# Layer 0 projections on fp32 operands in place of pairs of a high and a low part

## The chip, the cores and the metric

The kernel runs on 1 core of a Trainium2 chip. The metric is the device time of one execution in microseconds (us), lower is better. The kernel before was timed in 3 runs.

## What is computed

A trunk of two layers on 1024 tokens of width 1024, all of it fp32. Layer 0 mixes the tokens by sparse attention: each query keeps the 256 keys that a small indexer scores highest, and attends over a low-rank latent of those. Layer 1 mixes them by a gated MLP over chunks of 128 tokens. A SwiGLU block follows each. The change lies at the start of layer 0:

```python
h = modulate(rmsnorm(x, norm_mix_g[layer]), sh1, sc1)
proj = h @ w_in
q     = proj[..., :1024]                 # 8 heads x 128
c_kv  = rmsnorm(proj[..., 1024:1280], g_kv)
q_idx = proj[..., 1280:1792]             # 8 index heads x 64
k_idx = layernorm(proj[..., 1792:1856], g_kidx, b_kidx)
w_idx = proj[..., 1856:1864] * (8 ** -0.5 * 64 ** -0.5)
score = sum over heads of relu(q_idx . k_idx) * w_idx, causal
_, idx = lax.top_k(score, 256)
```

`modulate` scales and shifts h by two vectors that come from a product of the conditioning vector with `mod_w`.

## The kernel before

`trunk` (L111) runs on one core. A scheduler fixes the order of the instructions on each engine; tables at the head of the file give the order in which the source offers them. Tensors lie transposed, features on the 128 partitions: h is 8 tiles k (KT) of 128 features by 1024 tokens, worked on in two chunks `ch` of 512 tokens (CW). Buffers: `pg` has 37 pages of 128x1024 fp32, `wsp` has 8 for weights, `wrp` has 2 (tag `wr`) for raw weights and for the tiles `md` of the conditioning product.

Four projections multiply h, and all use one scheme. A weight tile is loaded raw by `split_w` (L145; SP issues the load, L149). ACT rounds it to a high part in fp32r (L154), and POOL or DVE subtracts to get the low part (L155). `norm_k` (L297) makes h for one k and chunk: DVE multiplies by the reciprocal root (L299), ACT scales and shifts (L301), ACT rounds to the high part (L303), and DVE for even k, POOL for odd k, subtracts for the low part (L304). A product is then three matmuls in `mm3` (L162): high by high (L165), high by low (L166), low by high (L167). "A step" here is one weight tile against one k and one chunk. Low by low is left out.

- **kw**, index keys and index weights, 72 columns: `kw_mm` (L392), 8 x 2 = 16 steps, weight tile `wi`.
- **qi**, index queries, 4 column tiles: `qi_mm` (L396) and the second half of `q_fin` (L427). 8 x 4 = 32 steps of 512 columns for chunk 1, and 32 of 256 columns for chunk 0, whose first 256 tokens keep all their keys. The weight comes in 4 tiles `wqi`.
- **c**, the latent: `ckv_chunk` (L477), 2 x 2 x 8 = 32 steps, weights `wc` (`wc_load`, L440).
- **q**, attention queries: `q_proj` (L460), 8 heads x 2 x 8 = 128 steps, weights `wq` (`q_load`, L450).

The order. BEG (L51) lists the front: loads of x (`x`), statistics (`s`), conditioning dot products (`m`, `mod_dot` L216: a load, then DVE in L232 or POOL in L221), h of chunk 0 and 1 (`a`, `b`), weights (`i`, `q`). There kw and qi run as tiles of h come. Then `idx_scores` (L617) makes index scores of blocks of 128 queries on PE (`lg_ps`, L633 and L634), DVE, ACT and POOL. SEQ (L41) mixes them with two groups of top-256 searches, `search` (L680). A search halves an interval again and again: DVE and ACT count scores above a threshold (L692, L690), DVE adds up and sets the next one (L694, L695); a high half of the bits, ending in `hikey`, comes ahead of a low half. FO (L42) lists the side work, q and c. `pump` (L520) deals it out between the index scores by RATE (L44), and what is left runs after them, mixed with `k_ps` and `v_ps` (keys and values of a head from the latent). The attention follows (`s_ps`, the scores), which needs the searches' results as a mask (`bias`, L750), then the output projection and the rest of the trunk, all of it with `mm3` or its like.

Of the kernel before, what the change touches and what calls it, by code (L numbers as in the profile page):

```python
# [8 lines left out]
F32 = mybir.dt.float32  # L9
# [10 lines left out]
P = 128  # L20
D = 1024
T = 1024
KT = 8
CW = 512
# [30 lines left out]
QWR = 1  # L55
SQPL = ((1, 2),)
PIN = 1
# [53 lines left out]
def trunk(ctx, tc, xT, c, modT, vec, kgb, w_idx, w_q, w_a, wuk, wuv, wo, wg, wu, wd,  # L111
          bwu, bwv, bwo, bws, bbs, outT):
    nc = tc.nc
    PE, DVE, ACT, POOL, SP = nc.tensor, nc.vector, nc.scalar, nc.gpsimd, nc.sync

    cst = ctx.enter_context(tc.tile_pool(name="cst", bufs=1))
    pg = ctx.enter_context(tc.tile_pool(name="pg", bufs=37))
    wrp = ctx.enter_context(tc.tile_pool(name="wrp", bufs=2))
    wsp = ctx.enter_context(tc.tile_pool(name="wsp", bufs=8))
# [6 lines left out]
    def page(name, dt=F32):  # L126
        return pg.tile([P, 1024], dt, name=name, tag="pg")

    def t2(name, dt=F32):
        return tmp.tile([P, CW], dt, name=name, tag="t2")  # L130

    def pa(name):
        return psa.tile([P, CW], F32, name=name, tag="pa")
# [4 lines left out]
    def hl(name, full=False):  # L138
        t = pg.tile([P, 2, CW], F32R, name=name, tag="pg")
        return (t[:, 0, :], t[:, 1, :], t) if full else (t[:, 0, :], t[:, 1, :])  # L140

    def f(ap):
        return ap.bitcast(F32)

    def split_w(src, n, name, pool=None, eng=None, rpool=None, pin=False):  # L145
        pl_, tag = pool or (wsp, "ws")
        rp, rtag = rpool or (wrp, "wr")
        r = rp.tile([P, 1024], F32, name=name + "r", tag=rtag)
        d = SP.dma_start(r[:, :n], src)  # L149
        if pin:  # L150
            tc.keep_in_program_order(d)
        h = pl_.tile([P, 1024], F32R, name=name + "h", tag=tag)
        l = pl_.tile([P, 1024], F32R, name=name + "l", tag=tag)
        ACT.copy(h[:, :n], r[:, :n])  # L154
        (eng or DVE).tensor_sub(l[:, :n], r[:, :n], f(h[:, :n]))  # L155
        return h, l

    def kslices(hl, n, w=P):
        h, l = hl
        return [(h[:, k * w:(k + 1) * w], l[:, k * w:(k + 1) * w]) for k in range(n)]  # L160

    def mm3(ps, st, mv, first, last, run=False):  # L162
        sh, sl = st
        mh, ml = mv
        PE.matmul(ps, sh, mh, start=first, stop=False, skip_group_check=run)  # L165
        PE.matmul(ps, sh, ml, start=False, stop=False, skip_group_check=run)  # L166
        PE.matmul(ps, sl, mh, start=False, stop=last, skip_group_check=run)  # L167
# [44 lines left out]
    modv = [cst.tile([P, 48], F32, name=f"modv{l}") for l in range(2)]  # L212
    asc = [[cst.tile([P, KT], F32, name=f"asc{l}{s}") for s in range(2)] for l in range(2)]
# [41 lines left out]
    def rstd_bcast(xs, n_feat, acc=None, sqs=None, mid=None, pp=None, sqp=None, bst=BST, order=range(KT)):  # L255
        pp = pp or pb
        st = pp("st")
        if sqp is not None:
            acc, sqs = sqp
            xs = [xs[k] for k in order]  # L260
            sqs = [sqs[k % len(sqs)] for k in range(KT)]
        elif acc is None:
            acc = t2("acc")
        for k, x in enumerate(xs):
            if k == 0:
                ACT.activation(acc, x, AF.Square)
            else:
                sq = sqs[k] if sqs else t2("sq")
                ACT.activation(sq, x, AF.Square)
                DVE.tensor_add(acc, acc, sq)  # L270
        v = sm.tile([P, 8], F32, name="var")
        for b in range(4):
            pe_st = PE.matmul(st[:, b:b + 1], acc[:, b * P:(b + 1) * P], ones[:, 0:1], start=True, stop=True)
        if mid is not None:
            next(mid)
        DVE.tensor_scalar(v[:, :4], st[:, :4], 1.0 / n_feat, EPS, op0=ALU.mult, op1=ALU.add)
        y = rsqrt_small(v[:, :4], 4)
        rb = pp("rb")
        if bst:
            for b in range(4):  # L280
                pe_rb = PE.matmul(rb[:, b * P:(b + 1) * P], y[:, b:b + 1].to_broadcast([P, P]), ident, start=True, stop=True)
            pe_chain[:] = [pe_st, pe_rb]
            return rb
        dg = tmp.tile([P, CW], F32, name="dg", tag="wt", bufs=2) if DGW else t2("dg")
        DVE.tensor_mul(dg.rearrange("p (b t) -> p b t", b=4), ident[:, None, :].to_broadcast([P, 4, P]),
                       y[:, :4, None].to_broadcast([P, 4, P]))
        pe_rb = PE.matmul(rb, ones, dg, start=True, stop=True)
        pe_chain[:] = [pe_st, pe_rb]
        return rb
# [4 lines left out]
        h = [sqpg[c][:, i * CW:(i + 1) * CW] for c in (ch, 2) for i in range(2) if c in sqpg]  # L294
        return h[0], [h[1]] + ([h[2 + ch]] if len(h) > 2 else [])

    def norm_k(x, rb, a, sh, k):  # L297
        xr = t2("xr")
        DVE.tensor_mul(xr, x, rb)  # L299
        h = t2("hf")  # L300
        ACT.activation(h, xr, AF.Identity, scale=a[:, k:k + 1], bias=sh[:, k:k + 1])  # L301
        hi, lo = hl("h")
        ACT.copy(hi, h)  # L303
        (POOL if k % 2 else DVE).tensor_sub(lo, h, f(hi))  # L304
        return hi, lo

    def norm_chunk(xp, ch, a, sh):
        cs = slice(ch * CW, ch * CW + CW)
        rb = rstd_bcast([x[:, cs] for x in xp], D)
        return [norm_k(xp[k][:, cs], rb, a, sh, k) for k in range(KT)]  # L310

    x0 = [page("x0") for _ in range(KT)]
    rbs = page("rbs")
    acc0 = page("acc0")
    sq0 = [page("sq0") for _ in range(2)]
# [3 lines left out]
    def x_load(ch):  # L319
        for k in range(KT):  # L320
            SP.dma_start(x0[k][:, ch * CW:(ch + 1) * CW], xT[k, :, ch * CW:(ch + 1) * CW])
# [39 lines left out]
    wis, wqi = [], [None] * KT  # L361
    h0 = [[None] * KT for _ in range(2)]
    with tc.issue_after(silu.ins):
        sq_table()
    for t in BEG:
        if t[0] == "x":
            x_load(int(t[1]))
        elif t[0] == "s":
            x_stat(int(t[1]))
        elif t[0] == "c":  # L370
            c_load()
        elif t[0] == "m":
            mod_first(int(t[1]))
        elif t[0] in "ab":
            k, ch = int(t[1]), int(t[0] == "b")
            cs = slice(ch * CW, ch * CW + CW)
            h0[ch][k] = norm_k(x0[k][:, cs], rbs[:, cs], asc[0][0], modv[0][:, 0:8], k)
        elif t[0] == "i":
            wis += kslices(split_w(w_idx, 8 * 72, "wi", pool=(pg, "pg"), rpool=(pg, "pg")), KT, 72)
        else:  # L380
            hl_ = split_w(w_q[int(t[1])], 1024, "wqi", eng=POOL, pool=(pg, "pg"), rpool=None if QWR else (pg, "pg"))
            wqi[2 * int(t[1]):2 * int(t[1]) + 2] = [kslices((hl_[0][:, q * CW:(q + 1) * CW], hl_[1][:, q * CW:(q + 1) * CW]), 4) for q in range(2)]
    kwp = [psa.tile([P, CW], F32, name="kw_ps", tag="pa") for _ in range(2)]
    qip = {(i, 0): pa("qi_ps") for i in range(QPA)}
    for i in range(4):
        qip[i, 1] = pb("qi_ps")
    Q0 = 256

    def q_in(hlk, ch):
        return [t[:, Q0:] for t in hlk] if ch == 0 else hlk  # L390

    def kw_mm(k):  # L392
        for ch in range(2):
            mm3(kwp[ch][:72], wis[k], h0[ch][k], k == 0, k == KT - 1)

    def qi_mm(i, ch, k):  # L396
        n = CW if ch else CW - Q0
        mm3(qip[i, ch][:, :n], wqi[k][i], q_in(h0[ch][k], ch), k == 0, k == KT - 1)

    for k in range(KT):  # L400
        if k < KWF:
# [4 lines left out]
    for k in range(KWF, KT):  # L406
        kw_mm(k)
# [19 lines left out]
    def q_fin():  # L427
        for (i, ch), p in qip.items():
            for k in range(K1, KT):
                qi_mm(i, ch, k)  # L430
            q_out(i, ch, p)
        for i in range(QPA, 4):
            p = pa("qi_ps")
            for k in range(KT):
                mm3(p[:, :CW - Q0], wqi[k][i], q_in(h0[0][k], 0), k == 0, k == KT - 1)
            q_out(i, 0, p)

    wc = []

    def wc_load():  # L440
        wc[:] = [kslices(split_w(w_a[8 + i], 1024, "wc", eng=POOL, pin=PIN), KT) for i in range(2)]

    q_d = drm.tile([NH, P, T], F32, name="q_d")
    o_d = drm.tile([NH, P, T], F32, name="o_d")
# [3 lines left out]
    WQ = {}  # L448

    def q_load(h):  # L450
        if h < NH:
            WQ[h] = kslices(split_w(w_a[h], 1024, "wq", eng=POOL, pin=PIN and h == 0), KT)

    gate = [None]

    def pe_step(p, w, mv, k):
        with (tc.issue_after(gate[0].ins) if gate[0] is not None else ExitStack()):
            mm3(p, w[k], mv[k], k == 0, k == KT - 1)

    def q_proj(h):  # L460
        w = WQ[h]
# [79 lines left out]
    if QF:  # L541
        q_fin()
    knat = page("knat")
    kn = knat[:, :NB * 72].rearrange("p (b d) -> p b d", b=NB)
    for ch in range(2):
        p = pa("kn_ps")
# [5 lines left out]
    mv = cst.tile([P, NB, 2], F32, name="mv")  # L552
# [21 lines left out]
    for ch in range(2):  # L574
        p = pa("kT_ps")
# [22 lines left out]
    for qbs in ((3, 2, 1, 0), (5, 4), (7, 6)):  # L598
        t = pg.tile([P, 2048], BF16, name="bias", tag="pg")
        o = 0  # L600
        for qb in qbs:
            bias[qb] = t[:, o:o + (qb + 1) * P]
            n = wide.get(qb, (qb + 1) * P)
# [4 lines left out]
    for qb in range(2):  # L608
        n = (qb + 1) * P
# [947 lines left out]
    for ch in F1:  # L1557
        if ch is None:
            continue
        cs = slice(ch * CW, ch * CW + CW)  # L1560
        rb = rstd_bcast([x[:, cs] for x in x1], D, sqp=sq_get(ch), order=SQO[ch], pp=pa, bst=FB[ch])
# [4 lines left out]
        for k in range(KT):  # L1566
            o = page("o")[:, :CW]
            x, fg = x1[k][:, cs], V[:, V_FIN + k:V_FIN + k + 1]
# [69 lines left out]
```

## Time and profile before

| | |
|---|---|
| 3 runs: median (lowest to highest) | 2643.21 us (2641.03 to 2648.29) |
| the profiled execution: its time, its span | 2644.98 us, 2643.0 us |
| PE, PE weight loads, DVE, ACT, POOL busy | 90%, 73%, 83%, 47%, 53% of the span |
| granted PE clock, mean | 0.948 of full speed |
| DMA | 328.65 MB, mean 124 GB/s |

The shares are means over stages with different limits. The part up to about 575 us is layer 0's attention, where the change is; the rest is the output projection, layer 1 and the two SwiGLU blocks. An fp32r matmul of 512 columns shows a duration of some 0.39 us but the next one starts 0.23 us later: they are pipelined, and the spacing is the cost. One core runs, so there is no other core to compare with.

### The profile page before, as it was taken

The numbers are of one execution on the slowest core, as the hardware profiler recorded it, in microseconds if no ns is written. First come the engines' busy times: TensorE is split into PE (matmuls) and PEld (weight loads), VectorE is DVE, ScalarE is ACT, GpSimd is POOL, SyncE is SP. The second block draws the span as 40 slices with busy tenths as digits, with TensorE's granted clock in tenths as the row PEclk, the third lists the DMA queues.
The fourth block names the chain that finished last, engine by engine and source line by source line (L and its number), as shares of the span: only waits on it lengthen the run. The fifth ranks groups of instructions, "written<-read, shape, count | busy, mean of one in ns | idle before, by whom it ended". The sixth has DMA issues, their size and how long they took to land.

```text
span 2643.0 us, 31759 instructions
## 1 busy us (share of the span) xinstructions
PE 2375.1 (90%) x10542; PEld 1934.4 (73%) x10542; DVE 2191.0 (83%) x3457; ACT 1245.9 (47%) x2278; POOL 1399.1 (53%) x993
## 2 busy tenths in 40 slices
PE   6979688998889999899988989988998999998996
PEld 5757577776677888777766877866776888886785
DVE  7799988799898887799879688899878656569986
ACT  5577785655533333343355454533454333333334
POOL 4342243365755554656646556575466444456663
PEclk7989788999899999999999999988989999998998
DMA  6001265645264453631122343363132222253121
GB/s 244 26 32 70 98 206 159 222 143 164 73 223 159 164 179 136 239 136 56 56 96 71 110 145 124 126 255 127 48 112 92 96 76 92 76 209 134 40 96 64
DMA packets 133924, 328.65 MB, mean 124 GB/s; under 512 B 14080, under 2 KB 30720, under 8 KB 133760
## 3 DMA queue, kind: packets, MB, share of 16 engines
q1 hardware_dynamic: 130432, 318.22, 34.5%
q0 software_dynamic: 3328, 8.39, 1.1%
q8 instruction: 84, 1.38, 0.2%
q14 instruction: 80, 0.66, 0.1%
HBM read 253.16 MB, written 73.40 MB: 124 GB/s over the span
## 4 chain that ended last, share of the span: by engine, by line
PE 44%; DVE 27%; issue 6%; DMA 6%; ACT 3%; POOL 2%; SPq 0%; DVEq 0%; POOLq 0%; ACTq 0%
PE p L1194 8%; PE p L1195 8%; PE p L1196 8%; PE d_ps L165 3%; PE d_ps L167 3%; PE d_ps L166 3%; DVE x L944 3%; DVE wst L1050 2%; DVE gm L1050 2%; DVE ms L957 1%; DVE md L232 1%; DVE wst L1174 1%; DVE sqp L270 1%; DMA zg<-z_d 1%; PE z_ps L166 1%
## 5 line engine op out<-in xcount | busy, mean ns | idle before, releaser
L1195 PE MATMUL p<-mv,wst 128*128 128x512 f32 x1232 | 487.4, 396 | 18.0 <-DVE mv L959 17.2
L1194 PE MATMUL p<-mv,wst 128*128 128x512 f32 x1232 | 486.8, 397 | 15.7 <-DVE uv L1229 8.1
L1196 PE MATMUL p<-mv,wst 128*128 128x512 f32 x1232 | 483.6, 393 | 0.6 <-DVE wst L1174 0.6
L1172 POOL TENSOR_TENSOR wsum<-wgu 128x512 f32<-128x512 f32 x208 | 300.4, 1445 | 318.3 <-DVE wst L1174 221.4
L165 PE MATMUL d_ps<-gm,wst 128*128 128x512 f32 x952 | 384.9, 405 | 68.4 <-DVE x L944 43.1
L167 PE MATMUL d_ps<-gm,wst 128*128 128x512 f32 x952 | 378.7, 400 | 7.5 <-DVE wst L1050 6.9
L166 PE MATMUL d_ps<-gm,wst 128*128 128x512 f32 x952 | 381.4, 401 | 0.4 <-DVE gm L1050 0.2
L1195 PEld LDWEIGHTS p<-mv,wst 128*128 128x128 f32 x1232 | 234.9, 191 | 73.6 <-DVE mv L959 23.8
L1194 PEld LDWEIGHTS p<-mv,wst 128*128 128x128 f32 x1232 | 235.2, 191 | 71.2 <-DVE uv L1229 8.4
L1173 ACT CAST wst<-wsum 128x512 fp32r<-128x512 f32 x260 | 160.7, 621 | 255.1 <-PE p L1196 117.1
L165 PEld LDWEIGHTS d_ps<-gm,wst 128*128 128x128 f32 x952 | 184.7, 194 | 120.1 <-ACT wst L1049 39.8
L1196 PEld LDWEIGHTS p<-mv,wst 128*128 128x128 f32 x1232 | 234.7, 191 | 49.6 <-DVE wst L1174 1.2
L1174 DVE TENSOR_TENSOR wst<-wsum,wst 128x512 fp32r<-128x512 f32 x208 | 203.7, 981 | 51.7 <-ACT wst L1173 50.9
L167 PEld LDWEIGHTS d_ps<-gm,wst 128*128 128x128 f32 x952 | 184.6, 194 | 49.6 <-DVE wst L1050 8.5
L166 PEld LDWEIGHTS d_ps<-gm,wst 128*128 128x128 f32 x952 | 184.9, 194 | 41.1 <-DVE gm L1050 2.1
L944 DVE SCALAR_TENSOR_TENSOR x<-d_ps,modv,x 128x512 f32<-128x512 f32 x252 | 185.0, 740 | 33.9 <-PE d_ps L167 33.9
L1050 POOL TENSOR_TENSOR gm<-graw,gm 128x512 fp32r<-128x512 f32 x108 | 166.8, 1555 | 75.7 <-ACT gm L1049 67.0
L1049 ACT CAST wst<-wraw 128x512 fp32r<-128x512 f32 (+1 forms) x216 | 124.1, 595 | 171.4 <-PE d_ps L167 157.7
L1050 POOL TENSOR_TENSOR wst<-wraw,wst 128x512 fp32r<-128x512 f32 (+1 forms) x54 | 78.7, 1457 | 145.2 <-ACT wst L1049 145.2
L1050 DVE TENSOR_TENSOR wst<-wraw,wst 128x512 fp32r<-128x512 f32 (+1 forms) x162 | 148.6, 922 | 8.0 <-ACT wst L1049 8.0
L1049 ACT CAST gm<-graw 128x512 fp32r<-128x512 f32 x204 | 118.9, 618 | 73.4 <-DVE wst L1050 23.0
L232 DVE SCALAR_TENSOR_TENSOR md<-md,cact 128x1024 f32<-128x1024 f32 x89 | 130.2, 1465 | 9.7 <-DMA md<-modT 9.5
(389 smaller groups left out, 5668.4 us busy)
## 6 DMA issues: line engine op xcount, KB each, us to landing
md<-modT SPq DMA_DIRECT2D x96, 512.0 KB, 4.7
wgu<-wg SPq DMA_DIRECT2D x56, 512.0 KB, 3.6
wgu<-wu SPq DMA_DIRECT2D x56, 512.0 KB, 4.4
g_d<-uv SPq DMA_DIRECT2D x88, 256.0 KB, 2.0
graw<-g_d SPq DMA_DIRECT2D x44, 512.0 KB, 7.2
wraw<-wd SPq DMA_DIRECT2D x64, 256.0 KB, 6.3
x_d<-x SPq DMA_DIRECT2D x48, 256.0 KB, 2.0
x<-x_d SPq DMA_DIRECT2D x24, 512.0 KB, 7.2
```

The source lines that it names most:

```text
L165: PE.matmul(ps, sh, mh, start=first, stop=False, skip_group_check=run)
L166: PE.matmul(ps, sh, ml, start=False, stop=False, skip_group_check=run)
L167: PE.matmul(ps, sl, mh, start=False, stop=last, skip_group_check=run)
L944: DVE.scalar_tensor_tensor(xk[:, cs], ps, gate, (xk[:, cs] if src is None else src), op0=ALU.mult, op1=ALU.add)
L1049: ACT.copy(t[:, 0, :n], s)
L1050: e.tensor_sub(t[:, 1, :n], s, f(t[:, 0, :n]))
L1172: SUM_ENG[j].tensor_tensor(s, o[0], o[1], op=o[2])
L1173: ACT.copy(t[:, 0], s)
L1174: LO_ENG[j].tensor_sub(t[:, 1], s, f(t[:, 0]))
L1194: PE.matmul(ps, sh, mh, start=k == 0, stop=False)
L1195: PE.matmul(ps, sh, ml, start=False, stop=False)
L1196: PE.matmul(ps, sl, mh, start=False, stop=k == 3)
```

## The change

Weight tiles of the four projections are loaded once and used as fp32 (`raw_w`), h is written by ACT as fp32 into 8 pages `h_all`, and each step is one `PE.matmul` on fp32 operands in place of `mm3`. The roundings and subtractions for them (L154, L155, L303, L304) are gone, and so is the raw buffer in `wrp` for `wq`, `wc` and `wqi`: a weight tile takes one buffer of `wsp` or `pg` in place of a raw and two parts. `norm_chunk`, which nothing calls, goes too. The rest of the trunk keeps `mm3`.

```diff
+    def raw_w(src, n, name, pool=None, pin=False):
+        pl_, tag = pool or (wsp, "ws")
+        r = pl_.tile([P, 1024], F32, name=name, tag=tag)
+        d = SP.dma_start(r[:, :n], src)
+        if pin:
+            tc.keep_in_program_order(d)
+        return r
+
+    def slices(t, n, w=P):
+        return [t[:, k * w:(k + 1) * w] for k in range(n)]
...
-    def norm_k(x, rb, a, sh, k):
+    def norm_k(x, rb, a, sh, k, ch):
         xr = t2("xr")
         DVE.tensor_mul(xr, x, rb)
-        h = t2("hf")
+        h = h_all[k][ch]
         ACT.activation(h, xr, AF.Identity, scale=a[:, k:k + 1], bias=sh[:, k:k + 1])
-        hi, lo = hl("h")
-        ACT.copy(hi, h)
-        (POOL if k % 2 else DVE).tensor_sub(lo, h, f(hi))
-        return hi, lo
+        return h
...
+    h_all = [page("h") for _ in range(KT)]
+    h_all = [(t[:, :CW], t[:, CW:]) for t in h_all]
...
-            wis += kslices(split_w(w_idx, 8 * 72, "wi", pool=(pg, "pg"), rpool=(pg, "pg")), KT, 72)
+            wis += slices(raw_w(w_idx, 8 * 72, "wi", pool=(pg, "pg")), KT, 72)
...
-            hl_ = split_w(w_q[int(t[1])], 1024, "wqi", eng=POOL, pool=(pg, "pg"), rpool=None if QWR else (pg, "pg"))
+            w = raw_w(w_q[int(t[1])], 1024, "wqi", pool=(pg, "pg"))
...
-            mm3(kwp[ch][:72], wis[k], h0[ch][k], k == 0, k == KT - 1)
+            PE.matmul(kwp[ch][:72], wis[k], h0[ch][k], start=k == 0, stop=k == KT - 1)
...
-        mm3(qip[i, ch][:, :n], wqi[k][i], q_in(h0[ch][k], ch), k == 0, k == KT - 1)
+        PE.matmul(qip[i, ch][:, :n], wqi[k][i], q_in(h0[ch][k], ch), start=k == 0, stop=k == KT - 1)
...
-                mm3(p[:, :CW - Q0], wqi[k][i], q_in(h0[0][k], 0), k == 0, k == KT - 1)
+                PE.matmul(p[:, :CW - Q0], wqi[k][i], q_in(h0[0][k], 0), start=k == 0, stop=k == KT - 1)
...
-        wc[:] = [kslices(split_w(w_a[8 + i], 1024, "wc", eng=POOL, pin=PIN), KT) for i in range(2)]
+        wc[:] = [slices(raw_w(w_a[8 + i], 1024, "wc", pin=PIN), KT) for i in range(2)]
...
-            WQ[h] = kslices(split_w(w_a[h], 1024, "wq", eng=POOL, pin=PIN and h == 0), KT)
+            WQ[h] = slices(raw_w(w_a[h], 1024, "wq", pin=PIN and h == 0), KT)
...
-            mm3(p, w[k], mv[k], k == 0, k == KT - 1)
+            PE.matmul(p, w[k], mv[k], start=k == 0, stop=k == KT - 1)
```

The scheduler's order changes with it, at three places. First, PE at the front, from the first step of qi on; before:

```order
L165 MATMUL qi_ps<-h,wqih 128x256
L166 MATMUL qi_ps<-h,wqih 128x256
L167 MATMUL qi_ps<-h,wqil 128x256
L165 MATMUL qi_ps<-h,wqih 128x256
L166 MATMUL qi_ps<-h,wqih 128x256
L167 MATMUL qi_ps<-h,wqil 128x256
L165 MATMUL kw_ps<-h,wih 72x512
L166 MATMUL kw_ps<-h,wih 72x512
L167 MATMUL kw_ps<-h,wil 72x512
L165 MATMUL qi_ps<-h,wqih 128x256 x2
```

After (L403 is `qi_mm`, L399 is `kw_mm`):

```order
L403 MATMUL qi_ps<-h,wqi 128x256 x4
L399 MATMUL kw_ps<-h,wi 72x512 x2
L403 MATMUL qi_ps<-h,wqi 128x512 x4
...
L403 MATMUL qi_ps<-h,wqi 128x256 x2
L403 MATMUL qi_ps<-h,wqi 128x512 x4
L399 MATMUL kw_ps<-h,wi 72x512 x13
L440 MATMUL qi_ps<-h,wqi 128x256 x16
L553 MATMUL kn_ps<-ident,kw 128x72 x8
L463 MATMUL q_ps<-h,wq 128x512 x14
L582 MATMUL kT_ps<-ident,kdup 128x128 x8
```

Each step is one row in place of three, and 13 of kw's 16 steps now stand behind all steps of the first qi tiles; the 16 steps of the last two tiles (L440) follow, as they did.

Second, SP's queue at the front, from the first two tiles `md` on (`x_104` to `x_111` are the second halves of x); before:

```order
L354 DMA md<-modT 128x1024 x2
L149 DMA wir<-w_idx 128x576
L149 DMA wqir<-w_q 128x1024
L321 DMA x_104<-xT 128x512
...
L321 DMA x_111<-xT 128x512
L149 DMA wqir<-w_q 128x1024
L218 DMA md<-modT 128x1024 x2
L149 DMA wqir<-w_q 128x1024
L218 DMA md<-modT 128x1024 x2
L149 DMA wqir<-w_q 128x1024
L218 DMA md<-modT 128x1024 x10
L149 DMA wqr<-w_a 128x1024 x3
```

After:

```order
L359 DMA md<-modT 128x1024 x2
L161 DMA wi<-w_idx 128x576
L161 DMA wqi<-w_q 128x1024
L229 DMA md<-modT 128x1024 x2
L326 DMA x_104<-xT 128x512
...
L326 DMA x_111<-xT 128x512
L782 DMA wkr<-wuk 128x256
L782 DMA wvr<-wuv 128x512
L161 DMA wqi<-w_q 128x1024
L229 DMA md<-modT 128x1024 x4
L161 DMA wqi<-w_q 128x1024
L229 DMA md<-modT 128x1024 x4
```

Two tiles `md` now go ahead of the second half of x, the first small weights of the attention (`wkr`, `wvr`) come in here, and the loads of `md` are spread between the three later `wqi`, 4 and 4 and 4, where 2, 2 and 10 stood.

Third, PE behind the last index score (the last `lg_ps`); before:

```order
L634 MATMUL lg_ps<-kiL,qiB 128x512
L165 MATMUL c_ps<-h,wch 128x512
L166 MATMUL c_ps<-h,wch 128x512
L167 MATMUL c_ps<-h,wcl 128x512
...
L167 MATMUL q_ps<-h,wql 128x512
L165 MATMUL k_ps<-ch,rgw 128x512
L166 MATMUL k_ps<-cl,rgw 128x512
L167 MATMUL k_ps<-ch,rgw 128x512
```

After:

```order
L639 MATMUL lg_ps<-kiL,qiB 128x512
L463 MATMUL c_ps<-h,wc 128x512 x3
L463 MATMUL q_ps<-h,wq 128x512 x12
L284 MATMUL st<-ones,acc 128x1 x4
L463 MATMUL q_ps<-h,wq 128x512 x15
L292 MATMUL rb<-ident,rs_y 128x128 x4
L463 MATMUL q_ps<-h,wq 128x512 x10
L176 MATMUL k_ps<-ch,rgw 128x512
```

Between the last `lg_ps` and the first `s_ps` stand 93 steps of c and q before, and 88 after, with the same 12 matmuls of `k_ps` and 24 of `v_ps` among them; the other five steps have moved in ahead of the last `lg_ps`. On POOL, DVE and ACT nothing takes the place of the splits that are gone.

## Rows read from the trace of the kernel before

**Rows 1.** The page's chain that ended last, by engine.

```profile
PE 44%; DVE 27%; issue 6%; DMA 6%; ACT 3%; POOL 2%; SPq 0%; DVEq 0%; POOLq 0%; ACTq 0%
```

**Rows 2.** Windows by stage: us; busy (instructions) per engine; clock, DMA share, GB/s.

```profile
36.00:99.00 63.00, 52.39 (x246) 40.11 (x245) 48.39 (x65) 32.14 (x54) 33.78 (x15) 0.90 0.27 104
99.00:213.00 114.00, 94.48 (x399) 74.72 (x398) 96.93 (x249) 72.90 (x141) 39.37 (x38) 0.91 0.09 31
213.00:285.00 72.00, 70.62 (x328) 57.79 (x326) 68.06 (x184) 61.57 (x122) 21.34 (x15) 1.00 0.26 93
285.00:430.00 145.00, 101.48 (x552) 85.63 (x552) 133.01 (x361) 97.06 (x230) 47.79 (x43) 0.83 0.49 164
575.00:2643.00 2068.00, 1905.26 (x8194) 1545.24 (x8192) 1700.09 (x2264) 872.15 (x1517) 1178.93 (x805) 0.96 0.35 122
```

**Rows 3.** PE's timeline by marks: start us, us, operation, count, idle before it.

```profile
35.88 0.56 PE L165 MATMUL qi_ps<-h,wqih 128*128 128x256 f32 x1
92.46 0.39 PE L167 MATMUL kw_ps<-h,wil 128*72 128x512 f32 x1
93.17 0.28 PE L166 MATMUL qi_ps<-h,wqih 128*128 128x256 f32 x1
93.52 0.28 PE L166 MATMUL qi_ps<-h,wqih 128*128 128x256 f32 x1
211.74 0.39 PE L165 MATMUL c_ps<-h,wch 128*128 128x512 f32 x1
212.19 0.39 PE L167 MATMUL c_ps<-h,wcl 128*128 128x512 f32 x1
284.94 0.33 PE L165 MATMUL s_ps<-rgk,rgq 128*128 128x128 f32 x1
```

**Rows 4.** DVE's timeline: where group 1's high search ends.

```profile
282.46 0.16 DVE L695 SCALAR_TENSOR_TENSOR hikey<-need,thr 128x3 f32<-128x3 f32 x1
```

**Rows 5.** PE's timeline around the first fp32 product of 512 columns (L287).

```profile
637.14 0.39 PE L165 MATMUL d_ps<-gm,wst 128*128 128x512 f32 x1
637.36 1.02 PE L287 MATMUL rb<-dg,ones 128*128 128x512 f32 x2
637.82 0.79 PE L166 MATMUL d_ps<-gm,wst 128*128 128x512 f32 x1
638.45 0.39 PE L167 MATMUL d_ps<-gm,wst 128*128 128x512 f32 x1
```

**Rows 6.** All PE weight loads of line 287: durations in ns, smallest, median, largest.

```profile
L287 PEld LDWEIGHTS rb<-dg,ones x14: 186/188/190, 637.1 to 2617.0; 128*128 128x128 f32 x14
```

**Rows 7.** One PE group of the whole run: count | busy us, mean ns | idle before.

```profile
L165 PE MATMUL q_ps<-h,wqh 128*128 128x512 f32 x128 | 51.2, 400 | 0.1
```

**Rows 8.** DVE groups from 0 to 92 us.

```profile
L232 DVE SCALAR_TENSOR_TENSOR md<-md,cact 128x1024 f32<-128x1024 f32 x9 | 19.6, 2182 | 0.0
...
L304 DVE TENSOR_TENSOR h<-hf,h 128x512 fp32r<-128x512 f32 x8 | 8.3, 1037 | 3.4 <-ACT h L303 3.4
```

**Rows 9.** DVE's timeline at 34 us, POOL idle.

```profile
33.95 1.22 DVE L232 SCALAR_TENSOR_TENSOR md<-md,cact 128x1024 f32<-128x1024 f32 x1
```

**Rows 10.** POOL groups of the whole run that the change removes at the front.

```profile
L304 POOL TENSOR_TENSOR h<-hf,h 128x512 fp32r<-128x512 f32 x8 | 13.4, 1685 | 12.4 <-ACT h L303 12.4
L155 POOL TENSOR_TENSOR wqil<-wqir,wqih 128x1024 fp32r<-128x1024 f32 x4 | 10.3, 2580 | 23.0 <-ACT wqih L154 23.0
```

**Rows 11.** What SP's queue waited for from 0 to 92 us: total, times, longest.

```profile
SPq L149 <- POOL wqil L155: 29.4, 4, 15.8
```

**Rows 12.** POOL's timeline: the split of one `wq` tile.

```profile
244.59 2.37 POOL L155 TENSOR_TENSOR wql<-wqr,wqh 128x1024 fp32r<-128x1024 f32 x1 [6.97 <-ACT wqh L154]
```

**Rows 13.** DVE's timeline in that stretch: the same instruction of the search twice.

```profile
243.68 0.17 DVE L694 TENSOR_SCALAR need<-sgn 128x3 f32<-128x3 f32 x1
...
245.37 1.62 DVE L694 TENSOR_SCALAR need<-sgn 128x3 f32<-128x3 f32 x1
```

**Rows 14.** ACT groups from 213 to 285 us: the roundings of `wq`.

```profile
L154 ACT CAST wqh<-wqr 128x1024 fp32r<-128x1024 f32 x5 | 5.2, 1049 | 0.0
```

More of the change, by code (lines that the diff above doesn't have):

```diff
@@ L295, in sq_get @@
         return h[0], [h[1]] + ([h[2 + ch]] if len(h) > 2 else [])
-    def norm_k(x, rb, a, sh, k):
+    def norm_k(x, rb, a, sh, k, ch):
         xr = t2("xr")
         DVE.tensor_mul(xr, x, rb)
-        h = t2("hf")
+        h = h_all[k][ch]
         ACT.activation(h, xr, AF.Identity, scale=a[:, k:k + 1], bias=sh[:, k:k + 1])
-        hi, lo = hl("h")
-        ACT.copy(hi, h)
-        (POOL if k % 2 else DVE).tensor_sub(lo, h, f(hi))
-        return hi, lo
[L307 to L310, printed above, removed]
+        return h
     x0 = [page("x0") for _ in range(KT)]
+    h_all = [page("h") for _ in range(KT)]
+    h_all = [(t[:, :CW], t[:, CW:]) for t in h_all]
     rbs = page("rbs")
@@ L376, in trunk @@
             cs = slice(ch * CW, ch * CW + CW)
-            h0[ch][k] = norm_k(x0[k][:, cs], rbs[:, cs], asc[0][0], modv[0][:, 0:8], k)
+            h0[ch][k] = norm_k(x0[k][:, cs], rbs[:, cs], asc[0][0], modv[0][:, 0:8], k, ch)
         elif t[0] == "i":
-            wis += kslices(split_w(w_idx, 8 * 72, "wi", pool=(pg, "pg"), rpool=(pg, "pg")), KT, 72)
+            wis += slices(raw_w(w_idx, 8 * 72, "wi", pool=(pg, "pg")), KT, 72)
         else:
-            hl_ = split_w(w_q[int(t[1])], 1024, "wqi", eng=POOL, pool=(pg, "pg"), rpool=None if QWR else (pg, "pg"))
-            wqi[2 * int(t[1]):2 * int(t[1]) + 2] = [kslices((hl_[0][:, q * CW:(q + 1) * CW], hl_[1][:, q * CW:(q + 1) * CW]), 4) for q in range(2)]
+            w = raw_w(w_q[int(t[1])], 1024, "wqi", pool=(pg, "pg"))
+            wqi[2 * int(t[1]):2 * int(t[1]) + 2] = [slices(w[:, q * CW:(q + 1) * CW], 4) for q in range(2)]
     kwp = [psa.tile([P, CW], F32, name="kw_ps", tag="pa") for _ in range(2)]
@@ L387, in trunk, with q_in @@
     Q0 = 256
-    def q_in(hlk, ch):
-        return [t[:, Q0:] for t in hlk] if ch == 0 else hlk
+    def q_in(t, ch):
+        return t[:, Q0:] if ch == 0 else t
     def kw_mm(k):
         for ch in range(2):
-            mm3(kwp[ch][:72], wis[k], h0[ch][k], k == 0, k == KT - 1)
+            PE.matmul(kwp[ch][:72], wis[k], h0[ch][k], start=k == 0, stop=k == KT - 1)
     def qi_mm(i, ch, k):
         n = CW if ch else CW - Q0
-        mm3(qip[i, ch][:, :n], wqi[k][i], q_in(h0[ch][k], ch), k == 0, k == KT - 1)
+        PE.matmul(qip[i, ch][:, :n], wqi[k][i], q_in(h0[ch][k], ch), start=k == 0, stop=k == KT - 1)
     for k in range(KT):
```

## The prediction

> **What bounds the kernel now.** I read the chain that ended last first: PE carries 44% of it and DVE 27% [rows 1], so neither engine alone decides, and the stages must be read one by one. The windows [rows 2] and the marks on PE's timeline [rows 3] give them:
> - The front, from the first step of qi at 35.9 us to the last of kw at 92.7. The work there is 32 steps of qi and 16 of kw, 512 columns each, and 16 of 256. Steps of 512 columns take three spacings; two of them are 211.74 to 212.19, so a step costs 0.68 us. Three of 256 columns take 0.35 (93.17 to 93.52) [rows 3]. 48 x 0.68 + 16 x 0.35 = 38.2 us in 56.8 us: PE waits for a third of the time, for h.
> - The index scores, from 92.7 to 211.7. PE shows 94.5 of 114 us busy and DVE 96.9 [rows 2]; durations of pipelined matmuls overlap, so PE is less full than that.
> - The tail, from 211.7 to the first attention score `s_ps` at 284.9 [rows 3]: 73.2 us with PE busy 70.6 of 72 at full clock [rows 2]. PE is the bound.
> - Beside it run the searches on DVE (68.1 of 72) and ACT (61.6 of 72) [rows 2]. Group 1's high search ends at 282.5 [rows 4].
> - From 285 to 430, searches, masks and attention share DVE, which is busy 133 of 145 us, while PE has 101 and a clock of 0.83 [rows 2]. DVE is the bound.
> - From 575 on PE is busy 1905 of 2068 us [rows 2]. Nothing there changes; it starts earlier or later by what the stages before it give.
>
> **The price of a step.** The trace has an fp32 product of 512 columns, at line 287: it appears as two matmul records [rows 5]. It starts at 637.36, and the L167 two behind it at 638.45. The L166 between them costs one spacing of 0.22 (637.14 to 637.36), so the product ends at 638.23: 0.87 us, or 0.43 per record. I take 0.86 at 512 columns and 0.43 at 256, half of it. Its weight load is 0.19 us [rows 6], which a record of 0.43 can hide. So a step rises from 0.68 to 0.86 us, +0.18, and one of 256 columns from 0.35 to 0.43, +0.08. There are 128 steps of q [rows 7], 32 of c, 32 of qi and 16 of kw: 208 x 0.18 + 32 x 0.08 = 40 us more PE work in all, though a third of the instructions. This speaks against the change; where it lands decides. By the Trainium skill, FP8 and Floating Point Precision, section TensorE Precision Notes, true fp32 takes four passes through the array; four spacings of 0.227 would be an estimate of 0.91 us, 4.4 us more over the tail's 88 steps, and the gain below would fall to about 5. The row shows two records of 0.43 and that is what I use.
>
> **Front.** Gone are, on DVE, 8 subtractions of L304, 8.3 us [rows 8]; on POOL 8 of L304, 13.4, and 4 of `wqil`, 10.3 [rows 10]; and ACT's roundings. POOL's work costs DVE too: L232 takes 2.18 us on average here [rows 8] and 1.22 with POOL idle [rows 9], so 9 x 0.96 = 8.6 us. SP's queue held the next `wqir` until POOL had read a raw buffer, four times, up to 15.8 us [rows 11], with the loads of `md` queued behind it; that wait ends with the ring. DVE, which paced h, is relieved by about 17 us. PE's 18.6 us of waits shrink to 8.6 by the 10 us of added work alone, so 17 is enough to fill them, and PE becomes the bound: the new work is 48 x 0.86 + 16 x 0.43 = 48.2 us. It starts at 37.1: two loads of `md` now go ahead of the second half of x, and I put one more L232 of 1.2 us [rows 9] in the way. I add 1.5 for a first 3 us at half clock (0.90 is the mean here [rows 2]). Last kw at 86.8 in place of 92.7: **-6**. Bounds: 0 if h still comes no faster than now, -9 if the clock is full and the start not later.
>
> **Index scores.** 67 steps of 512 and 16 of 256 before are now 72 and 16 (five moved in from the tail): 72 x 0.86 + 16 x 0.43 = 68.8 us against 51.2, +17.6. With at most 94.5/114 of 119 us busy, 98.6, PE comes to at most 116 of 119 us: nearly full, just inside. DVE loses four splits' worth of blocking. I take 0, so the last `lg_ps` ends at about 205.7; bounds -5 (DVE leads) and +8 (PE, matched badly to the evictions it feeds, leads).
>
> **Tail.** Here nothing hides PE. 93 steps x 0.68 = 63.3 us become 88 x 0.86 = 75.7: +12.4, so 85.6 us from the last index score, and the first `s_ps` at 291, **+6** against 284.9.
>
> **Searches.** They gain what PE loses. They begin 6 us earlier. Five splits of `wq` fall in this stretch; one runs on POOL from 244.59 for 2.37 [rows 12], and the search's L694 on DVE beside it takes 1.62 in place of 0.17 [rows 13]: 5 x 1.45 = 7.3 us of a chain in which each threshold waits for the last. ACT, counting for the same chain, loses 5.2 us of roundings [rows 14], of which I take half as already beside other work. Together -16: the high search ends at 266.5. By the Trainium skill, SBUF — State Buffer, section SBUF: two separate sides, VectorE and GpSimd share a port that one of them locks for a whole instruction; it would allow up to 5 x 2.4 = 12 us here, 5 more than the rows (an estimate, from the section's rule and the row's 2.4 us); the one pair read shows 1.45, which I keep.
>
> **Where it comes out.** DVE then has 16 us of its search work done before 285, and its share of the next stage is 133/145 = 0.92, so that stage would end 14.7 us earlier if DVE alone bound it. It cannot use all of it: the attention starts 6.4 later on PE and its passes follow in order. 14.7 less 6.4 is **8 to 9 us earlier** at 430 and, with nothing changed behind, at the end. Against the profiled execution's 2645.0 that is 2636; it lies 1.8 above the median of the runs, so the median comes to **2634**. On its own this forecast spans 5 to 14 us of gain, 2629 to 2638, chiefly by the front's 0 to -9 and the index scores' -5 to +8. The loads lose nothing: the same bytes, and each weight takes one buffer in place of three.
>
> **Rivals.**
> 1. No change, -5 to +5 us, about 2641. PE's lateness in the tail and a full PE in the index scores use up what DVE gains: the mask of the first attention pass is not what the first `s_ps` waits for, and DVE has nothing to do with its lead until PE delivers. For: the later stages are PE's. Against: DVE's 133 of 145 us.
> 2. Slower, on PE: the fp32 steps are not 0.86 us in a row, because here each has a new weight tile in two loads, while line 287 repeats one; with the loads not hidden a step costs 0.86 + 2 x 0.19 = 1.24. The tail would then take 88 x 0.38 = 33 us more than I say, and the index scores, full but for 3 us, 72 x 0.38 - 3 = 24: 2691. To lose the 8.5 us of the forecast and 7.9 more, each of the 160 steps must cost 0.10 more: it decides from 0.96 us per step, where the time is 2651. With half of the loads hidden, 1.05 us, it is 2661 to 2664. Against: 0.19 fits under 0.43, and the records of `mm3` hide a load of the same length under 0.23.
> 3. A larger gain, 14 to 22 us, 2622 to 2629: DVE's whole lead counts, and PE's lateness does not, because `s_ps` finds a mask waiting and the passes run without the waits for DVE that they have now.
> 4. The fp32 products run as one record each at fp32r's pace, so the change doesn't do what it says and PE gains 2 x 0.23 per step instead. The two records of line 287 [rows 5] all but exclude it.
>
> **Chances.** The forecast 0.50, rival 1 0.22, rival 2 0.15, rival 3 0.11, rival 4 0.02. A measurement of this kernel tells about 0.3%, 7.9 us, from no change. The forecast's middle, 8 to 9, lies on that border: a little over half of it counts as faster, I take 0.32 of the 0.50, which with rivals 3 and 4 gives 0.45. The rest of the forecast, 0.18, rival 1 and 0.02 of rival 2 below its point make 0.42 for the same, and 0.13 is left for slower. The range goes from 2623, within rival 3, to 2650, past rival 1 and up to the point where rival 2 decides.
>
> **What would show it.** Right: steps of q spaced 0.86 us, two records each; the last kw at about 87, the last `lg_ps` at 206, the first `s_ps` near 291, `hikey` of group 1 near 267; L694 at 0.2 us throughout; the stage from 285 on shorter by 14 us on DVE. Wrong: steps at 1 us or more; a last `lg_ps` past 214; a first mask that comes no earlier; or gaps on DVE before 291 that hand the lead back.

## The result and the profile after

The change is faster, by less than one per cent: median 2628.35 us (2621.82 to 2638.73, 10 runs) against 2644.67 us (2640.96 to 2648.29, 10 runs), ratio 0.9942 with the interval 0.993 to 0.9955. A second series of both gave 2629.75 and 2642.62, ratio 0.9955 (0.994 to 0.997). That is 13 to 16 us. The profiled execution of the change, 2638.73 us, is the slowest of its ten; its span is 2637.0.

The windows by stage [rows 2]: stretch, us; PE, PE weight loads, DVE, ACT, POOL busy (instructions); granted clock, DMA share, GB/s.

```profile
36.00:99.00 63.00, 63.00 (x183) 32.82 (x182) 34.32 (x79) 23.01 (x40) 10.48 (x9) 0.98 0.16 60
99.00:213.00 114.00, 99.16 (x317) 57.60 (x316) 88.10 (x216) 69.09 (x135) 28.41 (x30) 0.94 0.09 32
213.00:285.00 72.00, 72.00 (x196) 34.52 (x196) 66.88 (x207) 57.17 (x117) 8.38 (x8) 1.00 0.24 86
285.00:430.00 145.00, 116.29 (x618) 97.25 (x617) 128.84 (x361) 101.03 (x238) 53.91 (x46) 0.86 0.50 167
```

PE is now busy all of 36 to 99, where it waited a third of the time. POOL falls from 33.8 to 10.5 us there and from 21.3 to 8.4 from 213 to 285. PE's timeline of the change at the same marks [rows 3], and the end of the high search on DVE [rows 4]:

```profile
78.50 7.03 PE L399 MATMUL kw_ps<-h,wi 128*72 128x512 f32 x16
85.45 7.17 PE L440 MATMUL qi_ps<-h,wqi 128*128 128x256 f32 x32
...
212.16 0.40 PE L639 MATMUL lg_ps<-kiL,qiB 128*128 128x512 f32 x1
212.39 2.74 PE L463 MATMUL c_ps<-h,wc 128*128 128x512 f32 x6
214.97 10.46 PE L463 MATMUL q_ps<-h,wq 128*128 128x512 f32 x24
225.27 0.95 PE L284 MATMUL st<-ones,acc 128*128 128x1 f32 x8
...
295.34 0.22 PE L176 MATMUL s_ps<-rgk,rgq 128*128 128x128 f32 x1
...
538.28 0.39 PE L176 MATMUL d_ps<-gm,wst 128*128 128x512 f32 x1
```

```profile
273.10 0.16 DVE L700 SCALAR_TENSOR_TENSOR hikey<-need,thr 128x3 f32<-128x3 f32 x1
...
413.80 0.41 DVE L755 TENSOR_SCALAR bias<-bias 128x1024 bf16<-128x1024 int16 x1
```

The 24 records of q from 214.97 to 225.27 are 12 steps: 0.858 us each, two records of 0.43. The last line of PE's timeline is a mark that all further readings use: the first matmul of the output projection, where layer 0's attention is over. In the kernel before it stands here:

```profile
548.46 0.39 PE L165 MATMUL d_ps<-gm,wst 128*128 128x512 f32 x1
```

A second profile of each gave 547.5 before and 538.0 after. So the attention ends 9 to 10 us earlier. Behind the mark both kernels run the same instructions, in the same order on DVE, ACT and SP, and on PE and POOL but for one that has changed places right behind it.

| mark, us | before, two profiles | change, two profiles | forecast |
|---|---|---|---|
| last kw | 92.5, 90.8 | 84.9, 84.5 | 86.8 (its end) |
| last index score | 211.5, 209.7 | 212.2, 214.6 | 205.7 |
| group 1's high search ends | 282.5, 280.7 | 273.1, 275.5 | 266.5 |
| first attention score | 284.9, 283.2 | 295.3, 297.8 | 291 |
| last mask (L750, then L755) | 430.2, 428.5 | 413.8, 416.1 | |
| output projection | 548.5, 547.5 | 538.3, 538.0 | 8 to 9 earlier |

### The profile page after: what moved, and what is told of

Its sections match the earlier page's. It is cut to its first block, busy times and chain, and to the rows that moved or that the text cites. A ratio compares the mean times of both kernels' runs of the same rounds, so it can differ in the third digit from the quotient of the medians.

```text
span 2637.0 us, 31201 instructions
## 1 busy us (share of the span) xinstructions
PE 2399.7 (91%) x10302; PEld 1890.6 (72%) x10302; DVE 2154.2 (82%) x3448; ACT 1223.1 (46%) x2247; POOL 1357.6 (51%) x971
## 4 chain that ended last, share of the span: by engine, by line
PE 48%; DVE 35%; issue 7%; DMA 5%; ACT 3%; POOL 2%; SPq 0%; DVEq 0%; ACTq 0%; POOLq 0%
PE p L1199 9%; PE p L1200 9%; PE p L1201 9%; DVE x L949 3%; DVE wst L1055 3%; PE d_ps L176 3%; PE d_ps L178 3%; PE d_ps L177 3%; DVE gm L1055 3%; DVE sc L697 2%; DVE wst L1179 2%; DVE md L243 2%; PE q_ps L463 2%; DVE ms L962 1%; PE qi_ps L403 1%
## 5 line engine op out<-in xcount | busy, mean ns | idle before, releaser
L1199 PE MATMUL p<-mv,wst 128*128 128x512 f32 x1232 | 485.6, 396 | 16.4 <-DVE uv L1234 8.1
L1054 ACT CAST gm<-graw 128x512 fp32r<-128x512 f32 x204 | 119.0, 618 | 71.4 <-DVE wst L1055 23.0
L243 DVE SCALAR_TENSOR_TENSOR md<-md,cact 128x1024 f32<-128x1024 f32 x89 | 119.7, 1347 | 6.9 <-DMA md<-modT 6.9
```

The source lines that it names most:

```text
L243: DVE.scalar_tensor_tensor(m, m, 1.0, cact, op0=ALU.mult, op1=ALU.mult, accum_out=dot)
L1054: ACT.copy(t[:, 0, :n], s)
L1199: PE.matmul(ps, sh, mh, start=k == 0, stop=False)
```

## The experiments

**The change once more.**

> The changed kernel once more, for a second profile and the spread of its times. Theory A (the gain is the searches' lead on DVE, and the later first attention score costs nothing): median 2622 to 2634; last kw near 85, last index score near 212, hikey of group 1 near 273, last lokey near 350, first attention score near 295. Theory B (the profile after, 2638.7, is typical of where the lead goes: some 4 to 5 us of it are given back behind 600 us): the second profile shows the same losses near 650 and near 1600 us and its time lies near 2636.

2629.75 us; the marks are in the table. At the mark the two profiles of the change agree to 0.3 us. Behind it this one is 7.4 us shorter, mostly at 600 to 750 and at 1600 to 1750 us, so single profiles say little about that stretch. The time is theory A's and not B's. That the later first attention score costs nothing, as A says, no second run of one kernel can show; the cheaper steps below speak against it.

**Cheaper steps, and dead splits, in a free order.** In the first, a step of q and c is three fp32r matmuls of operands rounded once; in the second and third, splits are made again and not used.

```diff
-            PE.matmul(p, w[k], mv[k], start=k == 0, stop=k == KT - 1)
+            for i in range(3):
+                PE.matmul(p, w[k], mv[k], start=k == 0 and i == 0, stop=k == KT - 1 and i == 2)
```

> The changed kernel, but each step of q and c is three fp32r matmuls on the same rounded operands, at 0.68 us in place of 0.86; a weight is rounded by ACT once and no low part is made or used, so the products are not the reference's (q and c come out three times as large, of rounded operands). Theory A: the tail is some 15 us shorter, the first attention score near 278 to 283, yet the time is within 4 us of the changed kernel's, because DVE's searches set the stage behind. Theory B (PE's added work is on the path, as the prediction subtracted it): 6 to 15 us faster than the changed kernel.

> The changed kernel with the splits of wq and wc made again (ACT's rounding, POOL's subtraction) and used by nobody; the products stay fp32. Theory A: five of POOL's subtractions block DVE's search again, 1.45 us each: hikey of group 1 near 280 to 282, the time 6 to 10 us over the changed kernel's. Rival (PE's tail sets the end of the stage, and the searches have slack): hikey later by the same, the time within 3 us of the changed kernel's.

```diff
+            w = raw_w(w_a[h], 1024, "wq", pin=PIN and h == 0)
+            dead(w, 1024)      # ACT.copy and POOL.tensor_sub into the ring's two buffers
```

> The changed kernel with the splits of h, wqi and wi made again at the front and used by nobody. Theory A: h comes as late as before, the last kw near 91 to 93, everything behind it 6 to 8 us later, the last index score near 219, the time 5 to 9 us over the changed kernel's. Rival (the lead of the front is lost in the index scores anyway, since the last index score stands at 212 in both kernels): the last index score within 3 us of 212, the time within 3 us of the changed kernel's.

Times: 2637.06, 2660.12 and 2643.01 us; marks: 540.2, 559.4 and 536.2. By their times the third supports theory A, 13 us lost. The marks say otherwise: it is 2 us ahead of the change at the projection, although its last index score is 8 to 11 us late (222.8). The scheduler had drawn another order: some 395 of PE's 2003 matmul records up to the mark stand elsewhere, most of them from 328 us on, and behind the mark DVE, ACT, POOL and SP differ as well; against the change's second profile it loses its 13 us from 1300 to 1950. The first kernel is reordered too, and so is the second; the dead pairs of weight tiles also take the ring's buffers. None of the three tells what it was made for.

**Orders held.** The next kernels carry a table of the order in which the change's (or the old kernel's) instructions stand on each engine, and an edge from each to the next. Added work is free to stand anywhere. With the change's table the orders come out as its own, but for what is added. A kernel with the edges alone was not run; the change itself stands in for it.

```diff
+    for k in at:                       # places in the recorded order, engine by engine
+        i = t[int(k)]
+        e = str(i.engine)
+        if e in last:
+            tc.add_manual_dep(i, last[e].name, info, reason="order")
+        last[e] = i
```

**The change's work in the old order.**

> The changed work in the order of before: on PE, DVE, ACT and POOL every instruction that both kernels have stands where it stood before (a step's one product where the first of its three stood), only SP's loads are left to the scheduler. The output projection's first matmul stands at 548.5 us before and at 538.0 and 538.3 in two profiles of the change. Theory A (work taken off DVE, ACT and POOL is the gain): it stands at 536 to 541, the time is 2624 to 2634. Theory C (the gain is the new order that the scheduler drew, not the work): it stands at 545 or later, the time is 2638 or more.

2650.38 us, ratio to before 1.0018 (1.0007 to 1.0029); mark 546.9. The last kw is early (85.6), the last index score earlier than in either kernel (203.5). Then the search from there to `hikey` takes 81.1 us, against 71.0 before. Its groups in that stretch, DVE and ACT (busy us, mean ns | idle before, what ended it):

```profile
L725 DVE TENSOR_SCALAR need<-sgn 128x3 f32<-128x3 f32 x30 | 5.0, 166 | 10.4 <-ACT sc L721 10.4
L500 ACT COPY qT<-q_ps 128x512 f32<-128x512 f32 x11 | 6.4, 582 | 16.4 <-PE q_ps L489 16.4
```

ACT copies q out of PSUM between the counts of the search. In the old order 11 copies stand there; with steps of 0.86 us their results come late, ACT waits 16.4 us with the next counts queued behind, and DVE waits 10.4 for the counts. In the kernel before the 11 copies wait 4.0 us, and the change's own order has 8 copies there and 2.0 us of such waiting. So the change's work, splits gone and steps dearer, gains only about 1 us at the mark in the old order: theory A falls as a full account, and most of the 9 to 10 us needs the order that the scheduler drew for dearer steps.

**Splits of wq and wc, order held.** Both halves, and POOL's alone.

```diff
+        free(ACT.copy(r, r))                 # in the kernel with both halves only
+        free(POOL.tensor_add(r, r, r))
```

> The changed kernel with every engine held to its order, and ten dead pairs put in, one per tile of wq and wc: ACT copies the tile onto itself, POOL adds it to itself (so the weights are twice the reference's). Theory A: the index search pays as before, hikey of group 1 is 8 to 10 us after where it stands in the change relative to the last index score (61 us), and the output projection begins 4 to 8 us later than 538; time 2633 to 2639. Theory C (the 21 us that the free run with dead splits lost were a worse order): nothing moves by more than 3 us at the output projection.

> The changed kernel with every engine held to its order and only POOL's half of the dead pairs: ten additions of a tile of wq or wc to itself (the weights are twice the reference's). The kernel with both halves begins the output projection at 550.6, of which 4.7 us are lost at the front where three of DVE's small instructions meet POOL. Theory P (POOL's blocking of DVE is the price of a split): 545 to 551, and L694's counterpart in the search takes more than 1 us five times. Theory R (ACT's rounding, in ACT's order ahead of the search's counting, is the price): within 3 us of 538.

2644.68 and 2643.32 us; marks 550.6 and 547.7: 12.4 and 9.6 us later than the change. From the last index score to `hikey`: 64.4 and 67.1 us, against 60.9 in both profiles of the change. The sum-up of counts in that stretch, in the kernel before, the change's second profile and POOL's half alone:

```profile
L694 DVE TENSOR_SCALAR need<-sgn 128x3 f32<-128x3 f32 x30 | 12.1, 403 | 0.0
```

```profile
L699 DVE TENSOR_SCALAR need<-sgn 128x3 f32<-128x3 f32 x30 | 5.4, 180 | 0.0
```

```profile
L729 DVE TENSOR_SCALAR need<-sgn 128x3 f32<-128x3 f32 x30 | 11.6, 387 | 0.0
...
L185 POOL TENSOR_TENSOR wq<-wq 128x1024 f32<-128x1024 f32 x4 | 7.6, 1895 | 26.3 <-DMA wq<-w_a 26.3
```

The same 30 instructions of 3 columns cost 12.1, 5.4 and 11.6 us: four of POOL's additions put back 6.2. Theory P holds for the search, with four long instructions where five were expected, and POOL's half alone brings the 9.6 us, 2.4 of them already at the first step of qi. The two kernels are no sum of halves, though. With both halves only one of three additions in that stretch meets the sum-up, which takes 7.0 us; the high search is 3.5 us longer, where theory A said 8 to 10, and the stretch from the last kw to the last index score takes 134.5 us (change 127.2 and 130.1). Both kernels also start late, the first step of qi at 40.5 and 38.2 in place of 35.8, of which more below. What ACT's rounding costs by itself was not tried.

**Splits of the front, order held.**

```diff
+        free(ACT.copy(r, r))
+        free(eng.tensor_add(r, r, r))        # h by DVE and POOL in turn, wqi by POOL, wi by DVE
```

> The changed kernel with every engine held to its order, and dead pairs at the front, for wi, the four wqi and the 16 pieces of h: ACT copies the piece onto itself, POOL or DVE adds it to itself (so these operands are twice the reference's). Theory A (a lead of the front is carried to the end): the last kw 6 to 9 us later than 85, the output projection 5 to 9 us later than 538, time 2634 to 2640. Rival (the stage from 285 on, which waits for other things, absorbs it): the last kw as late, the output projection within 3 us of 538, time within 4 us of 2630.

2641.61 us; first step of qi 42.1, 6 us late; last kw 100.9, 16 us late and 8 later than before, since each half now waits for the other; last index score 226.5, `hikey` 287.5, mark 542.6. Of 16 us at the front 12 to 14 arrive at the last index score and 4.6 at the projection: the attention stage gives most of it back, and the rival is nearer than theory A. The time is 12 to 13 us over the change's all the same; 4 to 5 of that are in the mark. Against the change's second profile 5.5 more are lost, all from 1600 on; against its first, nothing is lost behind the mark.

**Cheaper steps, order held.**

> The changed kernel with every engine held to its order, but a step of q and c is three fp32r matmuls on the same rounded operands at 0.68 us in place of one at 0.86, and ACT rounds each tile of wq and wc once (the products are not the reference's: three times as large, of rounded operands). Theory A: the tail from the last index score to the first attention score falls from 83 to 72 us or so, ACT's roundings make the search some 5 us longer, and the output projection begins within 3 us of 538: what PE's added work costs in the tail is not on the path. Theory B (PE's added work is on the path): the output projection begins 5 to 10 us earlier than 538.

2625.56 us, ratio to before 0.9936 (0.9921 to 0.9952); mark 527.5. Last kw to last index score 120.9 us (change 127.2 and 130.1), tail 77.6 (83.2). The projection is 10.5 to 10.8 us earlier than in the change, with ACT's ten roundings added: PE's dearer steps are on the path, theory B. It is no kernel to use, since it leaves the low parts out.

**The kernel before once more.**

> The kernel before once more, for a second profile. If its marks can be read to 1 us as those of the change can (538.0 and 538.3): last kw within 1 us of 92.5, last index score within 3 of 211.5, first attention score within 3 of 284.9, the output projection's first matmul within 1 us of 548.5. If the front's collisions between DVE and POOL are drawn anew in each execution: the last kw and all that follows differ by 2 to 5 us.

One run, 2646.49 us; its marks are in the table. They move together by 1.6 to 1.8 us from the front on and by 0.9 at the end.

**The last two heads' queries inside the attention pass.**

```diff
-    pump(1000)
+    q_need(5)
...
+        if u < NH:
+            q_need(min(u + 2, NH - 1))
```

> The changed kernel, but the last two heads' queries (32 steps, 27.5 us of PE) are made between the units of the first attention pass and no longer ahead of it; the scheduler draws its own order. Three fp32r matmuls per step brought the output projection from 538 to 527.5 by a tail shorter by some 6 to 11 us, so PE's tail is on the path: expected is a first attention score at 266 to 272, an output projection at 526 to 534 and a time of 2617 to 2626. If the first attention pass has no room on PE (101 to 116 of 145 us busy say it has), the output projection stays at 538 or later and the time at 2628 or more.

2668.17 us, ratio 1.0093 (1.0076 to 1.011): slower. The first attention score comes at 271.4 as planned, 24 us early, but the mark stands at 563.3, 25 late. The largest loss is between the third and fourth unit of the pass: the reciprocals of their sums (`rd`) stand 45.6 us apart, against 18.7 and 19.8 in the change. There PE waits 20 us for ACT, and ACT for DVE:

```profile
352.11 0.79 PE L176 MATMUL o_ps<-rgpT,rgv 128*128 128x512 f32 x1 [20.19 <-ACT rgpT L804]
```

```profile
351.47 0.59 ACT L804 CAST rgpT<-pt_ps 128x512 fp32r<-128x512 f32 x1 [6.59 <-DVE er L759]
```

Ahead of this cast ACT works off the last counts of the low search, until 344.9, and the cast is then released by L759, a step of the first mask on DVE. No copy of q stands in the way here. The scheduler has put the end of the search ahead of this unit, so the run shows what that order costs, and not whether the pass has room on PE. Of the versions that compute all of the reference, none tried is faster than the change.

**SP's wait at the front, taken away in the kernel before.**

```diff
-QWR = 1
+QWR = 0
```

> The kernel before with one table entry changed: the raw tiles of wqi go to pages and no longer to the two buffers of the ring that the conditioning tiles use; PE, DVE, ACT and POOL are held to the order of before, SP's loads are free. SP's queue then has no 15.8 us wait for POOL at the front. Prediction's step (the loads of md are queued behind that wait and h comes late by it): the last kw 2 to 6 us ahead of 91 to 92.5, the output projection 1 to 4 us ahead of 547.5 to 548.5. Rival (DVE and POOL set the pace of the front whatever SP does): the last kw within 1 us of 91 to 92.5, the output projection within 1 us, the time within 3 us of before.

2651.06 us, ratio 1.0024 (1.0013 to 1.0034); last kw 96.3, mark 551.1: neither forecast is met. Ten of the later loads of `md` are now issued by 31.5 us, where SP stood still from 20.8 to 32.3 with four of them issued. But the first step of qi starts at 41.0, 5 us late, and from there to the last kw it takes 55.2 us, as in the two profiles of before (56.6 and 55.2). The 5 us come with the edit: SP, free in its order, issues the first `wqi` at 15.1 in place of 8.6, and ACT, held to its own, waits for it ahead of the statistics of the second half of x. In the kernel before, and in this one:

```profile
15.94 1.04 ACT L154 CAST wqih<-wqir 128x1024 fp32r<-128x1024 f32 x1 [0.60 <-DMA wqir<-w_q]
```

```profile
21.15 1.04 ACT L180 CAST wqih<-wqir 128x1024 fp32r<-128x1024 f32 x1 [6.02 <-DMA wqir<-w_q]
```

So the test is not clean; as far as it goes, earlier loads of `md` did not shorten the front.

## Why the prediction came out as it did

The time forecast was 2634, 9 us faster; measured are 13 to 16, inside the range of 2623 to 2650; the two medians, 2628.35 and 2629.75, lie on the lower edge of the forecast's own 2629 to 2638. That the sum came out is in part luck: one term failed by 8 to 11 us, and two gains that were not in the forecast, in the low search and behind the mark, made up for it. By steps:

- **Price of a step**: 0.86 forecast, 0.858 measured, weight loads (0.19) hidden; rival 2 is out, and so is rival 4. The Trainium skill's four passes (FP8 and Floating Point Precision, TensorE Precision Notes), taken at 0.227 each, gave an estimate of 0.91, and the measured 0.858 decides.
- **Front**: -6 forecast, -7.5 measured (85.45 against 92.95 for the matmul behind the last kw; -6.3 in the second profiles), with PE busy throughout. The part given to SP was not borne out (last experiment, not a clean one). What of the lead reaches the mark is a third or less in the one kernel that tells: the held order carried 4.6 of 16. DVE's relief from POOL came as forecast: the nine products of `md` [rows 8] take 8.6 us less.

```profile
L243 DVE SCALAR_TENSOR_TENSOR md<-md,cact 128x1024 f32<-128x1024 f32 x9 | 11.0, 1227 | 0.0
```

- **Index scores**: this term failed. 0 was forecast, with bounds of -5 and +8; measured are +8 and +11 (119.0 and 118.9 to 127.2 and 130.1; the granted clock was 0.95 in the first of the change's profiles and 0.92 in the second). The dearer steps were taken to fill PE's waits, but 14.8 us of waits remain of 19.6 (127.2 us less 112.4 busy, against 119.0 less 99.4), so most of PE's added work came on top. The kernel with steps of 0.68 needs 120.9.
- **Tail**: +12.4 forecast, +9.8 measured (83.2 against 73.4).
- **Searches**: the high search was to shorten by 9.9 (7.3 for POOL's blocking, 2.6 for ACT) and did by 10.1 (71.0 to 60.9): 6.7 of it in the one line that was named, and POOL alone put 6.2 back. The named cause covers 5.2 of the 6.7, where 7.3 was forecast: four of the five removed splits meet the sum-up, and the rest stood beside work of POOL that stays but now falls elsewhere. ACT's 2.6 were not tested. The end of the high search came only 5 to 9 us earlier and not 16, since the last index score was not early. Not forecast is a second gain: the low search takes 77.3 us in place of 85.0 in both profiles of the change, with the attention's first score 22 us behind `hikey` in place of 2.5. That DVE is then free for the search is the likeliest reason; no run tests it.
- **Stage behind the first attention score**: DVE was taken to bind it, and the profiles fit that. From that score to the mark DVE's work falls from 229.6 and 229.5 us to 207.4 in both profiles, as search work is done ahead; the time in which DVE does nothing stays, 34 and 35 us before, 36 and 33 in the change, and the stretch shrinks from 264 to 243 and 240 us, while PE's busy time falls by 2 to 4 only.
- **Sum**: the last mask is 12 to 16 us early, the projection 9 to 10, near the 8 to 9 forecast for the end of the stage. PE's lateness is not free: rival 3 has about the size of the result, but its reason is refuted by the held order with cheaper steps, 10.5 to 10.8 us ahead at the mark. With the order held, the parts are about -12.4 (splits of wq and wc, some of it an accident) and -4.6 (front) against +10.6 (PE), -6; they need not add up to the 9 to 10, as the order was redrawn between the two kernels.
- **Behind the mark**: 3 to 7 us of the medians' difference arise there, with the same instructions in the same order. In the kernels with this order, medians less marks range from 2090 us (the change) to 2104 (its work in the old order). The profiles don't agree on a place, and whether it belongs to the change stays open.
- **Clock**: a rival that the prediction has not. The runs' mean granted clock is 0.957 to 0.960 in the change's two series and 0.951 in the kernel before, and from 36 to 99 us it rose from 0.90 to 0.98. It isn't enough by itself: POOL's half alone has 0.958 and the time of before. How much of the gain it makes, behind the mark above all, was not separated.

By the Trainium skill (SBUF — State Buffer, SBUF: two separate sides) the port pair that VectorE and GpSimd share goes to one instruction for its whole length. The trace agrees: the slow L694 of [rows 13] ends at 246.99, with POOL's subtraction of [rows 12] at 246.96. The 12 us were an upper bound: an instruction that comes later in POOL's waits only for the rest of it, and one split of the five met none.

## What to carry to other kernels

Removing work from an engine that is not the bound can still pay through those that it blocks; look for the same small instruction at two durations, and count it. Where a scheduler draws the order, a changed time is not yet the effect of the changed part: take a mark behind the stage, compare the orders, and hold the order for the experiment. Work that waits in an engine's queue delays what stands behind it there: copies out of PSUM that waited 16.4 us held up the counts of the search, and counts of the search held up a unit of the attention for 20. So free time on PE alone doesn't say that a step can be moved there.

## Not expected of the hardware

Less than half a microsecond decided 4.7. In the kernel with both dead halves DVE runs 0.4 us later at the front than in the change; POOL's next product of `md` starts at 33.89, just ahead of two of DVE's last small steps for the second half of x:

```profile
33.94 2.31 DVE L292 SCALAR_TENSOR_TENSOR rs_t<-rs_t,var 128x4 f32<-128x4 f32 x1
...
36.28 2.26 DVE L294 SCALAR_TENSOR_TENSOR rs_y<-rs_t,rs_y 128x4 f32<-128x4 f32 x1
```

In the change's second profile DVE is done before POOL's product starts at 33.86:

```profile
33.49 0.16 DVE L261 SCALAR_TENSOR_TENSOR rs_t<-rs_t,var 128x4 f32<-128x4 f32 x1
...
33.68 0.16 DVE L263 SCALAR_TENSOR_TENSOR rs_y<-rs_t,rs_y 128x4 f32<-128x4 f32 x1
```

The first step of qi then starts at 40.5 in place of 35.8. An order can be right by a hair; what these 4.7 us come to at the mark was not measured by themselves.
